# Input projection of a two-layer step: two load queues, x turned one feature tile at a time, the norm applied from PSUM

## The chip, the cores and the metric

The kernel runs on one core of a Trainium2 chip. Times are device microseconds (us) of one execution. The kernel before takes 849.61 us, the median of three runs (848.19 to 850.14).

The engines have short names here: PE is TensorE (matrix products and transposes), PEld its weight loads, DVE is VectorE, ACT is ScalarE, POOL is GpSimd, and SP is the engine that issues loads and stores. An engine that issues a load does so in its own order of instructions: what stands behind the issue waits until it is out.

## The reference, cut to what matters

One step of a model with two layers, all in float32. There are 128 context tokens (x_prompt) and 512 latent tokens (x_sample), each with 1024 features. Layer 0 is latent attention, layer 1 a gated chunk MLP. The change touches the first step of layer 0, the input projection:

```python
sh_c, sc_c, g_c = modulation(c_ctx, w_mod[layer], b_mod[layer])   # silu(cond) @ w_mod + b_mod
sh_l, sc_l, g_l = modulation(c, w_mod[layer], b_mod[layer])
hc = rmsnorm(xc, norm_g[layer]) * (1.0 + sc_c) + sh_c
hl = rmsnorm(xl, norm_g[layer]) * (1.0 + sc_l) + sh_l
proj = h @ w_in             # for hc and hl
c_q, c_kv, k_pe, z = split(proj, [512, 256, 64, 1024])
```

Behind it come the norms of c_q and c_kv, attention, the output projection, layer 1 and the final norm. None of them changes.

## The kernel before, in words

The 640 tokens are five token tiles of 128 (tile 0 is the prompt), the 1024 features eight feature tiles of 128. Large operands are split in two: a part H that is rounded to the type fp32r, and the rest L. A product is then three products of TensorE, one behind the other (`mm3`, L149 to L151: H by H, H by the other's L, L by H), a "triplet".

The order in the code around the change is this. SP issues the five tiles of x (`load_x`, L174) and between them seven small loads of rows (`load_rows`, L183): c, c_ctx, b_mod and some gains. TensorE turns the rows into columns (L201), and VectorE and ScalarE make silu(c) of them. Then come the pieces of w_mod: `PIECES` cuts the eight feature tiles into six pieces (four of one tile, two of two). `mod_piece` loads a piece with four loads (L231) and multiplies it with silu(c) (L236; the trace records each of these float32 products twice); `mod_cols` copies the result to SBUF (L249), turns it (L251) and makes from it the gain and the offset of each feature (`acol`, `modc`, L256 to L272). `load_tok` loads 832 columns of attn_w_in for one feature tile (L290) and splits them (L144 on ScalarE, L145 on VectorE).

Meanwhile x is normed: ScalarE squares and sums each tile (L300), VectorE and GpSimd form the root, VectorE scales the tile in place (L304), for the last tile ScalarE does (L306). Then TensorE turns all of x, 40 transposes of 128x128 (L311), and ScalarE copies them from PSUM to SBUF (L318; L315 and L316 for one tile). `h_piece` applies gain and offset to a feature tile (L330, in place) and splits it.

The loop at the end (L529) goes over the pieces. In each turn it prepares the next piece, and multiplies the present one: for each token tile the 512 columns of c_q (`tok_mm` with kv 0, 128x512), and for token tiles 0 and 1 the 320 columns of c_kv and k_pe too (kv 1, 128x320). The sums of kv 0 stay in PSUM banks 0 to 4, those of kv 1 go to banks 5 to 7. Behind the loop come the last piece, all kv 1 products of token tiles 2 to 4, and each tile's norm.

The order of each engine's instructions is fixed when the program is built: a scheduler interleaves what the code lists, and each engine then works its list off in order. Loads share eight signal lanes: a load that gets a lane which an earlier load holds is issued only when that one has landed.

Of the kernel before, what the change touches and what calls it, by code (L numbers as in the profile page):

```python
# [7 lines left out]
F32 = mybir.dt.float32  # L8
F32R = mybir.dt.float32r
AF = mybir.ActivationFunctionType  # L10
ALU = mybir.AluOpType
AX = mybir.AxisListType

P = 128
D = 1024
KD = D // P
NT = 5
TOK = NT * P
# [35 lines left out]
F_X = 0  # L54
F_Y = 5120
F_MOD = 10496
# [3 lines left out]
C_BMOD = 0  # L60
C_NG = 48
C_VG = 64
C_VB = 80
C_QG = 96
C_C = 100
# [29 lines left out]
def _program(tc, nc, i, o, sb, ps, dr):  # L95
    arR = sb.tile([P, R_N], F32R, name="arR")[:]
    arF = sb.tile([P, F_N], F32, name="arF")[:]
    ident = sb.tile([P, P], F32, name="ident")[:]
    cst = sb.tile([P, C_N], F32, name="cst")[:]
    silc = sb.tile([P, 16], F32, name="silc")[:]  # L100
    modc = sb.tile([P, 2, 24, 2], F32, name="modc")[:]
    acol = sb.tile([P, 2, 8, 2], F32, name="acol")[:]
# [17 lines left out]
    def F(a, n):  # L120
        return arF[:, a : a + n]
# [4 lines left out]
    def F3(at, cnt, **kw):  # L126
        return arF[:, at : at + cnt].rearrange("p (a b) -> p a b", **kw)

    arP = ps.tile([P, 4096], F32, name="arP")[:]
# [10 lines left out]
    V, S, T, G = nc.vector, nc.scalar, nc.tensor, nc.gpsimd  # L140

    def split(h, l, x):

        S.copy(h, x)  # L144
        V.tensor_tensor(l, x, h.bitcast(F32), ALU.subtract)  # L145
# [7 lines left out]
    def rstd(out, ss, n):  # L153

        V.tensor_scalar(out, ss, 1.0 / n, EPS, ALU.mult, ALU.add)  # L155
        G.tensor_tensor(out, out, nhalf, ALU.pow)  # L156
# [3 lines left out]
    def col(n=1):  # L160
        if scol[0] + n > 96:
            scol[0] = 0
        a = scol[0]
        scol[0] += n
        return st[:, a : a + n]
# [7 lines left out]
    def load_x(t):  # L173
        nc.sync.dma_start(F(F_X + t * D, D), x_src[t])  # L174

    def load_rows(name, at, n):
        src = i[name]
        src = (
            src.rearrange("(k p) -> k p", p=P)
            if len(src.shape) == 1  # L180
            else src.rearrange("a (k p) -> (a k) p", p=P)
        )
        nc.sync.dma_start(arF[at : at + n, F_MOD : F_MOD + P], src)  # L183

    load_x(0)
    load_rows("c", C_C, 8)
    load_rows("c_ctx", C_C + 8, 8)
    load_x(1)
    load_rows("b_mod", C_BMOD, 48)
    load_rows("norm_g", C_NG, 16)  # L190
    load_x(2)
    load_rows("mlp_v_norm_g", C_VG, 16)
    load_rows("mlp_v_norm_b", C_VB, 16)
    load_rows("attn_q_norm_g", C_QG, 4)
    load_x(3)
    load_x(4)
    make_identity(nc, ident)
    V.memset(nhalf, -0.5)

# [14 lines left out]

    PIECES = [(0, 1), (1, 1), (2, 1), (3, 1), (4, 2), (6, 2)]
    raw = Ring(F_MOD + 896, F_N)
    raw2 = Ring(F_X, F_X + 5120)

    def wmod(layer, c0, n, k0, nk):
        return i["w_mod"][layer, k0 * P : (k0 + nk) * P, c0 : c0 + n].rearrange(  # L220
            "(k p) n -> p k n", p=P
        )

    def mod_piece(k0, nk, second):


        n = 2 * nk * P
        for kk in range(2):
            a = (raw2 if second and kk else raw).take(4 * n)
            for part in range(2):  # L230
                nc.sync.dma_start(  # L231
                    F3(a, 4 * n, a=4)[:, :, part * nk * P : (part + 1) * nk * P],
                    wmod(0, part * D + k0 * P, nk * P, 4 * kk, 4),
                )
            for j in range(4):
                T.matmul(  # L236
                    arP[32 * j : 32 * j + 32, 3584 : 3584 + n],
                    s32[:, 4 * kk + j, :],
                    F(a + j * n, n),
                    start=kk == 0,  # L240
                    stop=kk == 1,
                    tile_position=(0, 32 * j),
                )
# [49 lines left out]
        wtok.append((R(w, TCOLS), R(w + TCOLS, TCOLS)))  # L293


    xnT = F3(F_Y, 5120, a=KD)
    for t in range(NT):
        x = F(F_X + t * D, D)
        ss = col()
        S.activation(F(F_Y + t * D, D), x, AF.Square, accum_out=ss)  # L300
        r = col()
        rstd(r, ss, D)
        if t < NT - 1:
            V.tensor_scalar(x, x, r, None, ALU.mult)  # L304
        else:
            S.activation(x, x, AF.Identity, scale=r)  # L306
    for t in range(NT):
        x = F(F_X + t * D, D)
        pt = arP[:, t % 3 * 1024 : t % 3 * 1024 + 1024]
        for k in range(KD):  # L310
            T.transpose(pt[:, k * P : (k + 1) * P], x[:, k * P : (k + 1) * P], ident)  # L311
        dst = xnT[:, :, t * P : (t + 1) * P]
        pt = pt.rearrange("p (k n) -> p k n", n=P)
        if t == 3:
            S.copy(dst[:, :4], pt[:, :4])  # L315
            V.tensor_copy(dst[:, 4:], pt[:, 4:])  # L316
        else:
            S.copy(dst, pt)  # L318

    def hT(k):  # L320
        a = R_HT + k * 1280
        return R(a, 640), R(a + 640, 640)

    def h_piece(k0, nk, t0=0, t1=NT):
        for k in range(k0, k0 + nk):
            h = xnT[:, k, :]
            H, L = hT(k)
            for c, a, b in ((1, t0 * P, P), (0, max(t0, 1) * P, t1 * P)):
                if a < b:
                    V.tensor_scalar(  # L330
                        h[:, a:b],
                        h[:, a:b],
                        acol[:, 0, k, c : c + 1],
                        modc[:, 0, k, c : c + 1],
                        ALU.mult,
                        ALU.add,
                    )
            sl = slice(t0 * P, t1 * P)
            split(H[:, sl], L[:, sl], h[:, sl])

# [3 lines left out]
    def tok_mm(t, ks, kv):  # L346
        out = PKV[t] if kv else PQ[t]
        sl = slice(512, TCOLS) if kv else slice(0, 512)
        for k in ks:
            mm3(  # L350
                out,
                [z[:, t * P : (t + 1) * P] for z in hT(k)],
                [z[:, sl] for z in wtok[k]],
                k == 0,
                k == KD - 1,
            )
# [167 lines left out]

    load_tok(0)
    mod_cols(*PIECES[0])
    h_piece(0, 1, 0, 2)
    h_piece(0, 1, 2, NT)
    for q, (k0, nk) in enumerate(PIECES):  # L529
        ks = range(k0, k0 + nk)  # L530
        if q + 1 < len(PIECES):
            mod_piece(*PIECES[q + 1], True)
            mod_cols(*PIECES[q + 1])
            h_piece(*PIECES[q + 1])
            for k in range(PIECES[q + 1][0], sum(PIECES[q + 1])):
                load_tok(k)
            for t in range(NT):
                tok_mm(t, ks, 0)
                if t < 2:
                    tok_mm(t, ks, 1)  # L540
    nc.sync.dma_start(kvg, i["attn_kv_norm_g"].partition_broadcast(P)[:, 0, :])
    for t in range(NT):
        tok_mm(t, ks, 0)
        tok_mm(t, ks if t < 2 else range(KD), 1)
        tok_norm(t)
        if t >= 2:
            tok_turn(t - 2)
# [822 lines left out]
    ss = [col(4) for t in range(NT)]  # L1370
# [14 lines left out]
    for t in range(NT):  # L1385
        x = x_half(t, 0)
# [6 lines left out]
    for t in range(NT):  # L1393
        x = x_half(t, 1)
# [75 lines left out]
```

## Time and profile before

| | |
|---|---|
| median of three runs | 849.61 us (848.19 to 850.14) |
| the profiled execution | 848.43 us |
| its span, first to last instruction | 846.6 us |
| busy in the span: PE / PEld / DVE / ACT / POOL | 812.5 / 741.5 / 640.6 / 408.9 / 18.1 us |
| bytes moved by loads and stores | 131.14 MB, mean 155 GB/s |

The profile is of one execution; its rows give starts from the beginning of the span. A busy time on PE is modelled: products are pipelined, and a product's row is longer than the step to the next one. So steps from start to start are used for prices. The granted clock is a share of 2.4 GHz: 1.00 is that, 0.50 is 1.2 GHz; where no change has been recorded yet, at the start, the view shows 1.00.

### The profile page before, as it was taken

What the parts mean: (1) busy time and instruction counts of PE and PEld (TensorE: products, weight loads), DVE (VectorE), ACT (ScalarE), POOL (GpSimd) and SP (SyncE); (2) the same over time, 40 slices, a digit from 0 to 9 for tenths busy, and PEclk for the clock granted to TensorE, in tenths of its full rate; (3) what the DMA queues carried; (4) which work ended last, traced back from release to release, by engine and by line L of the source; (5) the groups of instructions that cost most, each with busy time, mean ns of one, the idle gap of its engine ahead of it and who ended that gap; (6) DMA issues with size and microseconds to landing.
All of it is one profiled execution on the core that took longest, in us unless ns stands there. A gap on an engine that the chain in (4) does not pass through costs nothing.

```text
span 846.6 us, 12750 instructions
## 1 busy us (share of the span) xinstructions
PE 812.5 (96%) x4874; PEld 741.5 (88%) x4874; DVE 640.6 (76%) x1133; ACT 408.9 (48%) x720; POOL 18.1 (2%) x31
## 2 busy tenths in 40 slices
PE   4999999999999999999999979999999999889996
PEld 3779999999999998888878779999999999668886
DVE  3665997879899896568866778998888787775432
ACT  6344362867666783244323376455455454642111
POOL 1001000000000000000000000000000000000000
PEclk9999999999999999999999989999999999999999
DMA  9981574111223137456869467534425366762212
GB/s 282 298 277 33 168 227 152 26 51 60 85 76 100 37 117 271 133 174 202 264 209 289 136 216 243 174 119 140 156 83 173 104 210 200 227 196 87 63 64 74
DMA packets 115734, 131.14 MB, mean 155 GB/s; under 512 B 5564, under 2 KB 81880, under 8 KB 115416
## 3 DMA queue, kind: packets, MB, share of 16 engines
q1 hardware_dynamic: 115672, 130.32, 49.3%
q8 instruction: 38, 0.62, 0.3%
q14 instruction: 24, 0.20, 0.1%
HBM read 106.78 MB, written 23.52 MB: 154 GB/s over the span
## 4 chain that ended last, share of the span: by engine, by line
PE 70%; DVE 12%; DMA 9%; issue 4%; ACT 3%; POOL 1%; SPq 0%; POOLq 0%; DVEq 0%; ACTq 0%
PE arP L1200 19%; PE arP L149 13%; PE arP L151 13%; PE arP L150 13%; PE arP L736 6%; DVE arR L145 3%; DMA arF<-d_h 2%; PE arP L764 2%; DVE arF L485 2%; DMA arF<-in_mlp_w_in 2%; DMA arF<-d_t 1%; ACT arR L144 1%; PE arP L1245 1%; PE arP L236 1%; PE arP L1246 1%
## 5 line engine op out<-in xcount | busy, mean ns | idle before, releaser
L149 PE MATMUL arP<-arR 128*128 128x512 f32 (+3 forms) x840 | 299.2, 357 | 8.6 <-ACT arR L144 8.0
L150 PE MATMUL arP<-arR 128*128 128x512 f32 (+3 forms) x840 | 297.6, 354 | 2.1 <-DVE arR L145 2.1
L151 PE MATMUL arP<-arR 128*128 128x512 f32 (+3 forms) x840 | 295.9, 354 | 0.0
L144 ACT CAST arR<-arF 128x1024 fp32r<-128x1024 f32 (+5 forms) x199 | 166.0, 854 | 190.0 <-PE arP L1200 31.6
L145 DVE TENSOR_TENSOR arR<-arF,arR 128x512 fp32r<-128x512 f32 (+5 forms) x199 | 190.8, 974 | 52.2 <-ACT arR L144 50.5
L1200 PE MATMUL arP<-arR 128*128 128x320 f32 x1344 | 203.3, 312 | 4.6 <-ACT arF L1274 3.8
L1200 PEld LDWEIGHTS arP<-arR 128*128 128x128 f32 x1344 | 200.0, 190 | 5.3 <-ACT arF L1274 4.1
L149 PEld LDWEIGHTS arP<-arR 128*128 128x128 f32 x840 | 158.4, 189 | 30.4 <-ACT arR L144 11.2
L150 PEld LDWEIGHTS arP<-arR 128*128 128x128 f32 x840 | 158.9, 189 | 20.7 <-DVE arR L145 3.6
L151 PEld LDWEIGHTS arP<-arR 128*128 128x128 f32 x840 | 158.7, 189 | 19.4 <-issue 0.8
L485 DVE SCALAR_TENSOR_TENSOR arF<-arF,silc 128x512 f32<-128x512 f32 x112 | 77.7, 743 | 2.5 <-DMA arF<-in_w_mod 2.5
L145 DVE TENSOR_TENSOR arR<-arP,arR 128x512 fp32r<-128x512 f32 (+4 forms) x86 | 54.7, 685 | 11.8 <-ACT arR L144 11.6
L736 PE MATMUL arP<-arR 128*128 128x320 f32 (+1 forms) x360 | 54.5, 308 | 0.1
L144 ACT CAST arR<-arP 128x512 fp32r<-128x512 f32 (+4 forms) x86 | 45.9, 605 | 16.5 <-PE arP L151 11.3
L736 PEld LDWEIGHTS arP<-arR 128*128 128x128 f32 x360 | 51.9, 188 | 0.4 <-DVE arR L699 0.4
L752 ACT ACTIVATE arF<-arP,st 128x640 f32<-128x640 f32 (+1 forms) x40 | 28.0, 701 | 23.4 <-DVE st L751 22.6
L1381 DVE TENSOR_TENSOR arF<-arP,arF 128x512 f32<-128x512 f32 (+1 forms) x11 | 6.8, 638 | 33.1 <-PE arP L151 33.1
L756 ACT ACTIVATE arF<-arF,st 128x640 f32<-128x640 f32 (+1 forms) x40 | 28.9, 743 | 2.3 <-DVE st L755 1.9
L748 DVE TENSOR_REDUCE st<-arP 128x1 f32<-128x640 f32 (+1 forms) x40 | 28.1, 708 | 1.7 <-PE arP L736 1.0
L1383 ACT ACTIVATE arF<-arF 128x512 f32<-128x512 f32 (+1 forms) x11 | 6.5, 588 | 45.3 <-DVE arF L1382 45.3
L1278 ACT COPY arF<-arP 128x320 f32<-128x320 f32 x16 | 6.8, 425 | 39.6 <-PE arP L1200 39.6
L156 POOL TENSOR_TENSOR st<-st,nhalf 128x1 f32<-128x1 f32 x15 | 10.1, 671 | 643.5 <-DVE st L155 331.6
(154 smaller groups left out, 682.2 us busy)
## 6 DMA issues: line engine op xcount, KB each, us to landing
arF<-in_mlp_w_in SPq DMA_DIRECT2D x48, 512.0 KB, 4.4
arF<-in_w_mod SPq DMA_DIRECT2D x40, 512.0 KB, 4.5
arF<-in_mlp_w_o SPq DMA_DIRECT2D x32, 256.0 KB, 3.3
arR<-d_vh SPq DMA_DIRECT2D x8, 640.0 KB, 4.5
d_t<-arF SPq DMA_DIRECT2D x16, 320.0 KB, 2.9
arF<-d_t SPq DMA_DIRECT2D x16, 320.0 KB, 3.9
arF<-in_x_sample SPq DMA_DIRECT2D x8, 512.0 KB, 4.8
arF<-in_w_mod SPq DMA_DIRECT2D x16, 256.0 KB, 6.1
```

Of the source, the lines that this page charges most:

```text
L144: S.copy(h, x)
L145: V.tensor_tensor(l, x, h.bitcast(F32), ALU.subtract)
L149: T.matmul(out, a[0], b[0], start=start, stop=False)
L150: T.matmul(out, a[0], b[1], start=False, stop=False)
L151: T.matmul(out, a[1], b[0], start=False, stop=stop)
L485: V.scalar_tensor_tensor(acc[:, c, :], w, sc, acc[:, c, :], ALU.mult, ALU.add)
L736: T.matmul(p[:, n0 : n0 + n], a[:, qs], b[:, c0 : c0 + n], start=s0, stop=s1)
L748: V.tensor_reduce(c[:, 0:1], sc, AX.X if q == 0 else AX.XY, ALU.max)
L752: S.activation(pv, sc, AF.Exp, bias=c[:, 0:1], scale=SCALE, accum_out=c[:, 1:2])
L756: S.activation(pr, pr, AF.Identity, scale=c[:, 2:3])
L764: T.transpose(p[:, at : at + P], PR[q][:, kt * P : (kt + 1) * P], ident)
L1200: T.matmul(out, x, y, start=first and k + j == 0, stop=k == 3 and j == 2, skip_group_check=True,)
```

## The change

- The loads are spread over two queues. SP issues the five tiles of x first, one behind the other. ScalarE issues the seven loads of rows and the four loads of the first piece of w_mod, ahead of all its other work.
- Eight products of zeros (128x256) are put in front on TensorE.
- The squares of x go to PSUM instead of SBUF, and the second ring of load buffers (`raw2`) lies in the free part of F_Y instead of x's own place.
- x stays in SBUF as it was normed. `h_piece` turns one feature tile of all five token tiles (L318, 5 transposes) into banks 5 and 6 of PSUM. VectorE makes h from there (L330), ScalarE makes the rounded H from there too (L331), and VectorE subtracts the two for L (L332). The copies L315, L316 and L318 of before go.
- All kv 1 products, for all token tiles, come behind the loop, since banks 5 and 6 are in use during it.

```diff
-    def load_rows(name, at, n):
+    def load_rows(name, at, n, eng=nc.sync):
...
-        nc.sync.dma_start(arF[at : at + n, F_MOD : F_MOD + P], src)
-
-    load_x(0)
-    load_rows("c", C_C, 8)
-    load_rows("c_ctx", C_C + 8, 8)
-    load_x(1)
...
-    load_x(3)
-    load_x(4)
+        eng.dma_start(arF[at : at + n, F_MOD : F_MOD + P], src)
+
+    for t in range(NT):
+        load_x(t)
+    load_rows("c", C_C, 8, nc.scalar)
+    load_rows("c_ctx", C_C + 8, 8, nc.scalar)
...
+    load_rows("attn_q_norm_g", C_QG, 4, nc.scalar)
+
+    zero = F(F_Y, 256)
+    V.memset(zero, 0.0)
+    for _ in range(8):
+        T.matmul(arP[:, 2048:2304], zero[:, :P], zero, start=True, stop=True)
...
-    raw2 = Ring(F_X, F_X + 5120)
+    raw2 = Ring(F_Y + 1280, F_Y + 5120)
...
-                nc.sync.dma_start(
+                (nc.sync if second else nc.scalar).dma_start(
...
-        S.activation(F(F_Y + t * D, D), x, AF.Square, accum_out=ss)
+        S.activation(arP[:, t % 2 * D : t % 2 * D + D], x, AF.Square, accum_out=ss)
...
-    for t in range(NT):
-        x = F(F_X + t * D, D)
-        pt = arP[:, t % 3 * 1024 : t % 3 * 1024 + 1024]
-        for k in range(KD):
-            T.transpose(pt[:, k * P : (k + 1) * P], x[:, k * P : (k + 1) * P], ident)
-        dst = xnT[:, :, t * P : (t + 1) * P]
-        pt = pt.rearrange("p (k n) -> p k n", n=P)
-        if t == 3:
-            S.copy(dst[:, :4], pt[:, :4])
-            V.tensor_copy(dst[:, 4:], pt[:, 4:])
-        else:
-            S.copy(dst, pt)
...
-    def h_piece(k0, nk, t0=0, t1=NT):
+    def h_piece(k0, nk):
+
         for k in range(k0, k0 + nk):
-            h = xnT[:, k, :]
+            for t in range(NT):
+                at = 2560 + (t - 1) * P if t else 3072
+                T.transpose(
+                    arP[:, at : at + P],
+                    arF[:, F_X + t * D + k * P : F_X + t * D + (k + 1) * P],
+                    ident,
+                )
+            h = F(F_Y + k % 2 * TOK, TOK)
             H, L = hT(k)
...
-            split(H[:, sl], L[:, sl], h[:, sl])
+            for c, sl, p in (
+                (1, slice(0, P), arP[:, 3072 : 3072 + P]),
+                (0, slice(P, TOK), arP[:, 2560:3072]),
+            ):
+                g, s = acol[:, 0, k, c : c + 1], modc[:, 0, k, c : c + 1]
+                V.tensor_scalar(h[:, sl], p, g, s, ALU.mult, ALU.add)
+                S.activation(H[:, sl], p, AF.Identity, bias=s, scale=g)
+            V.tensor_tensor(L, h, H.bitcast(F32), ALU.subtract)
...
             for t in range(NT):
                 tok_mm(t, ks, 0)
-                if t < 2:
-                    tok_mm(t, ks, 1)
...
         tok_mm(t, ks, 0)
-        tok_mm(t, ks if t < 2 else range(KD), 1)
+        tok_mm(t, range(KD), 1)
```

The scheduler orders each engine's instructions anew. On TensorE, from the first piece of w_mod (L236) to the first products of the projection (L149, L150), there stood before:

```order
L236 MATMUL arP<-arF 32x256 x4
L311 MATMUL arP<-ident,arF 128x128 x8
L236 MATMUL arP<-arF 32x256 x4
L311 MATMUL arP<-ident,arF 128x128 x8
L251 MATMUL arP<-ident,arF 128x128 x2
L236 MATMUL arP<-arF 32x256 x4
L149 MATMUL arP<-arR 128x512
L236 MATMUL arP<-arF 32x256 x4
L150 MATMUL arP<-arR 128x512
L149 MATMUL arP<-arR 128x320
```

Here the four groups of L236 are the two halves of piece 0 and the two of piece 1; the first product stands ahead of the second half of piece 1, and all transposes of x (L311) are done before it. Now the same place reads (L238 is the product of a piece, L253 its transposes, L318 the transposes of x):

```order
L238 MATMUL arP<-arF 32x256 x8
L318 MATMUL arP<-ident,arF 128x128
L253 MATMUL arP<-ident,arF 128x128 x2
L238 MATMUL arP<-arF 32x256 x4
L318 MATMUL arP<-ident,arF 128x128 x2
L238 MATMUL arP<-arF 32x256 x4
L253 MATMUL arP<-ident,arF 128x128 x2
L318 MATMUL arP<-ident,arF 128x128 x2
L149 MATMUL arP<-arR 128x512
L150 MATMUL arP<-arR 128x512
L238 MATMUL arP<-arF 32x256 x4
L318 MATMUL arP<-ident,arF 128x128 x4
```

The first product has moved behind both halves of piece 1 and its transposes; six transposes of x stand ahead of it and 34 behind. On ScalarE the program began like this before, with the squares (L300), the evacuations of transposes (L318, L315), the scaling of the last tile (L306) and the splits (L144):

```order
L300 ACT_TABLE_LOAD
L300 ACTIVATE arF,st<-arF 128x1024 x3
L206 ACTIVATE st<-cst 128x16
L300 ACTIVATE arF,st<-arF 128x1024 x2
L318 COPY arF<-arP 128x8x128
L306 ACTIVATE arF<-arF,st 128x1024
L318 COPY arF<-arP 128x8x128 x2
L315 COPY arF<-arP 128x4x128
L318 COPY arF<-arP 128x8x128
L144 CAST arR<-arF 128x832
L144 CAST arR<-arF 128x256
```

Now it begins with eleven loads, of which the last five are:

```order
L183 DMA arF<-in_attn_q_norm_g 4x128
L233 DMA arF<-in_w_mod 128x4x128 x4
L301 ACT_TABLE_LOAD
L301 ACTIVATE arP,st<-arF 128x1024
L208 ACTIVATE st<-cst 128x16
L301 ACTIVATE arP,st<-arF 128x1024 x3
L144 CAST arR<-arF 128x832
L301 ACTIVATE arP,st<-arF 128x1024
L307 ACTIVATE arF<-arF,st 128x1024
L331 ACTIVATE arR<-arP,modc,acol 128x128
L144 CAST arR<-arF 128x832
L331 ACTIVATE arR<-arP,modc,acol 128x512
```

The squares stand behind the loads, the split of attn_w_in's first tile stands ahead of the last square, the evacuations are gone, and the scalings from PSUM (L331) have come in their place, with a split between the two of the first feature tile.

## Rows read from the trace of the kernel before

**Rows 1.** Busy time by stage: us, PE, PEld, DVE, ACT, POOL, PEclk, DMA share, GB/s

```profile
0.00:20.70 20.70, 9.85 (x68) 7.31 (x68) 7.53 (x26) 13.54 (x21) 3.91 (x11) 1.00 0.91 281
20.70:59.60 38.90, 38.90 (x231) 28.22 (x232) 26.20 (x65) 13.55 (x20) 0.40 (x1) 1.00 0.97 301
59.60:130.00 70.40, 69.82 (x475) 68.18 (x474) 57.48 (x110) 31.95 (x66) 3.25 (x5) 1.00 0.51 151
```

**Rows 2.** The chain of waits in order of time, head: start us, us, what

```profile
1.91 4.75 DMA arF<-in_x_sample
...
15.19 1.15 ACT arF L306
16.34 1.81 ACT arF L318 x2
...
19.55 1.10 ACT arR L144 x2
...
20.70 0.50 PE arP L149
```

**Rows 3.** Busy time by stretch, columns as in rows 1: the head, and around 490

```profile
0.00:4.00 4.00, 0.00 (x0) 0.00 (x0) 0.33 (x2) 1.28 (x1) 0.70 (x6) 1.00 0.51 150
4.00:8.00 4.00, 0.00 (x0) 0.00 (x0) 0.29 (x3) 2.30 (x4) 0.55 (x1) 1.00 0.96 330
8.00:12.00 4.00, 3.16 (x14) 2.63 (x15) 2.61 (x7) 1.53 (x4) 1.56 (x2) 1.00 0.86 281
...
490.00:492.00 2.00, 2.00 (x11) 1.68 (x10) 0.64 (x4) 0.60 (x1) 0.55 (x1) 1.00 1.00 401
```

**Rows 4.** DMA issues by line: count, KB each, median us to landing (13.2 to 15.3; 0 to 75)

```profile
arF<-in_w_mod SPq DMA_DIRECT2D x4, 256.0 KB, 5.3
...
arF<-in_attn_w_in SPq DMA_DIRECT2D x8, 416.0 KB, 6.9
```

**Rows 5.** SP in order of time: start us, us, line, what it issues

```profile
1.17 0.37 SPq L183 DMA_DIRECT2D arF<-in_c  x1
...
13.18 2.08 SPq L231 DMA_DIRECT2D arF<-in_w_mod  x4
```

**Rows 6.** TensorE in order of time: start us, us, line, operation

```profile
11.06 3.52 PE L311 MATMUL arP<-ident,arF 128*128 128x128 f32 x16
...
15.07 1.09 PE L311 MATMUL arP<-ident,arF 128*128 128x128 f32 x8
...
21.13 0.64 PE L236 MATMUL arP<-arF 128*32 128x256 f32 x8
...
22.94 0.39 PE L150 MATMUL arP<-arR 128*128 128x512 f32 x1
23.17 0.38 PE L251 MATMUL arP<-ident,arF 128*128 128x128 f32 x2
23.30 0.48 PE L151 MATMUL arP<-arR 128*128 128x512 f32 x1
23.62 0.31 PE L149 MATMUL arP<-arR 128*128 128x320 f32 x1
...
59.59 0.30 PE L149 MATMUL arP<-arR 128*128 128x320 f32 x1
```

**Rows 7.** Groups by shape, 0 to 20.7: count | busy us, mean ns | idle before

```profile
L300 ACT ACTIVATE arF<-arF 128x1024 f32<-128x1024 f32 x5 | 5.2, 1050 | 3.7 <-DMA arF<-in_x_prompt 2.4 <-DMA arF<-in_x_sample 1.4
...
L306 ACT ACTIVATE arF<-arF,st 128x1024 f32<-128x1024 f32 x1 | 1.1, 1150 | 0.2 <-POOL st L156 0.2
...
L330 DVE TENSOR_SCALAR arF<-arF,acol,modc 128x128 f32<-128x128 f32 x2 | 0.6, 344 | 0.0
...
L249 DVE COPY arF<-arP 128x256 f32<-128x256 f32 x1 | 0.4, 412 | 0.0
```

**Rows 8.** TensorE behind an idle stretch, and the granted clock there (columns as rows 1)

```profile
727.22 0.50 PE L149 MATMUL arP<-arR 128*128 128x512 f32 x1 [3.66 <-ACT arR L144]
...
728.00:730.00 2.00, 2.00 (x7) 1.52 (x6) 1.97 (x6) 2.00 (x7) 0.00 (x0) 0.50 0.53 152
```

More of the change, by code (lines that the diff above doesn't have):

```diff
@@ L182, in load_rows @@
         )
-        nc.sync.dma_start(arF[at : at + n, F_MOD : F_MOD + P], src)
-    load_x(0)
-    load_rows("c", C_C, 8)
-    load_rows("c_ctx", C_C + 8, 8)
-    load_x(1)
[L189 to L194, printed above, removed]
-    load_x(3)
-    load_x(4)
+        eng.dma_start(arF[at : at + n, F_MOD : F_MOD + P], src)
[3 more added lines that the diff above has]
+    load_rows("c_ctx", C_C + 8, 8, nc.scalar)
+    load_rows("b_mod", C_BMOD, 48, nc.scalar)
+    load_rows("norm_g", C_NG, 16, nc.scalar)
+    load_rows("mlp_v_norm_g", C_VG, 16, nc.scalar)
+    load_rows("mlp_v_norm_b", C_VB, 16, nc.scalar)
+    load_rows("attn_q_norm_g", C_QG, 4, nc.scalar)
[3 more added lines that the diff above has]
+        T.matmul(arP[:, 2048:2304], zero[:, :P], zero, start=True, stop=True)
     make_identity(nc, ident)
@@ L293, in load_tok @@
         wtok.append((R(w, TCOLS), R(w + TCOLS, TCOLS)))
-    xnT = F3(F_Y, 5120, a=KD)
     for t in range(NT):
@@ L322, in hT @@
         return R(a, 640), R(a + 640, 640)
-    def h_piece(k0, nk, t0=0, t1=NT):
+    def h_piece(k0, nk):
         for k in range(k0, k0 + nk):
-            h = xnT[:, k, :]
-            H, L = hT(k)
[L328 to L338, printed above, removed]
-            split(H[:, sl], L[:, sl], h[:, sl])
+            for t in range(NT):
[6 more added lines that the diff above has]
+            h = F(F_Y + k % 2 * TOK, TOK)
+            H, L = hT(k)
+            for c, sl, p in (
[6 more added lines that the diff above has]
+            V.tensor_tensor(L, h, H.bitcast(F32), ALU.subtract)
     PQ = [arP[:, t * 512 : (t + 1) * 512] for t in range(NT)]
@@ L526, in _program @@
     mod_cols(*PIECES[0])
-    h_piece(0, 1, 0, 2)
-    h_piece(0, 1, 2, NT)
+    h_piece(0, 1)
     for q, (k0, nk) in enumerate(PIECES):
```

## The prediction

> **What bounds the kernel now.** I read the busy time by stage first. Up to 20.7 us TensorE is busy for 9.85 us, and little of that is products of the projection; from 20.7 to 59.6 us it is busy for all 38.90 us, and from there to 130 us for 69.82 of 70.40 us [rows 1]. So the stretch that the change touches has two parts with different limits: a head in which TensorE waits, and a stretch in which nothing but its own work counts. The chain of waits names what the head waits for: after the loads come the scaling of the last token tile on ScalarE, three evacuations of transposed x, the casts of h, and then the first product at 20.70 us [rows 2]. A gain has to come out of the head; whatever TensorE has to do after 20.7 us costs its full time.
>
> The point to compare at is a product that both programs share. From the 128x320 product of token tile 1 at feature tile 6, which starts at 59.59 us [rows 6], TensorE's order is the same in both programs to the end, and those of the other engines join within the same few products. TensorE is almost never idle for the next 70 us [rows 1]. So the change in the time is the change in when that product starts. In both programs 34 triplets of 128x512 and 14 of 128x320 stand between the first product of the projection and it.
>
> **The first product: what has to land.** In the changed order TensorE reaches its first product only behind all products of pieces 0 and 1 with w_mod (before: without the second half of piece 1). SP issues the five x tiles and attn_w_in of feature tile 0 ahead of piece 1. So five x tiles of 128x1024 float32 (512 KB each), eight w_mod loads of 256 KB, one of 416 KB [rows 4] and 58 KB of rows have to be in: 5.20 MB. These are the same bytes that lie ahead of the end of piece 1 before, where its four loads were issued from 13.18 to 15.26 us and landed 5.3 us later at the median [rows 4, 5]: the last at about 20.1 us. The second queue moves issue times, not bytes. The DMA engines were already 96% busy from 4 to 8 us at 330 GB/s, with one queue, and had a dip to 281 GB/s from 8 to 12 us [rows 3], while x waited for its place. Two queues can fill that dip: 4 us x 49 GB/s = 0.2 MB, or 0.6 us. I take 19.4 us. Bounds: 0.60 MB by 4 us [rows 3], the other 4.60 MB at 330 GB/s and no delay from last byte to signal, gives 17.9 us; nothing gained gives 20.1 us.
>
> The Trainium skill ("DMA: Bandwidth & Descriptors", section "Issuing engines are not separate DMA queues") says that transfers from several engines end on the same 16 DMA engines and interleave, so that a second issuer saves only issue time. By that rule the landing stays near 20.1 us; the trace agrees so far as one queue reaches a share of 0.96 to 1.14.
>
> **From landing to the first product.** The half of piece 1 on TensorE 0.64 us [rows 6], the copy of its rows 0.41, two transposes beside it, the gain and offset columns about 0.2, the first 128x128 scaling on VectorE 0.34 [rows 7], then the same on ScalarE, which waits for VectorE's reading; no row has it, 0.27 to 0.4 by its neighbour on VectorE. With the hand-overs 2.2 us: first product at 21.6 us, against 20.70. Behind it the tiles of x_sample need the 128x512 scaling on both engines in turn, and ScalarE has a cast of 128x832 queued ahead of it: tile 1 starts some 2.2 us after tile 0, of which TensorE fills 1.6 with two products, a piece and transposes. Idle: 0.6 us.
>
> ScalarE's own chain is not last by this count. It issues 11 loads of about 0.4 us each [rows 5] from 0.74 us and waits for the second x tile (landed at 6.66 us before [rows 2]); then a table load, five squares of 1.05 plus read-out, one cast of 128x832 and one scaling of 1.15 [rows 7] bring it to 17.7 us, or 19.6 where x lands late, and it is needed at 21.0. The evacuations removed there (L315, L318) were on the path before [rows 2]; what is late next is the w_mod piece.
>
> **The dense stretch.** Before: 59.59 - 20.70 = 38.9 us. The products are the same. Gone are one half piece (0.6 us) and two transposes. Added are 34 transposes of x, 128x128, which before were done in the head. Their price stands in the trace: L150, two transposes, L151 take 22.94 to 23.62 us, where the two products alone take 0.46, so 0.11 us each at the full clock [rows 6]; 34 x 0.11 = 3.7 us. The stretch is 38.9 - 0.6 - 0.2 + 3.7 = 41.8 us. The 128x320 products of tiles 0 and 1 move from the loop to its end, at no cost or gain, since TensorE does as many of them by the shared point. The loop per feature tile is then 5 x 3 x 0.23 for products, 0.55 for transposes, about 1.2 for the piece and 0.22 for its transposes: 5.4 us, where its loads (1.44 MB at 330 GB/s) take 4.4 us. So loads stay hidden, as does the scaling on VectorE and ScalarE; if that cover fails once per piece by half a microsecond it costs 3 us.
>
> Sum: 19.4 + 2.2 + 0.6 + 41.8 = 64.0 us, against 59.6: **+4.4 us** before the clock. Each microsecond of landing moves it by one.
>
> **The clock.** The eight products of zeros run at the start, from about 1.2 us, and are done by 8 us; nothing waits for them. What they could buy is the full clock. Before, the transposes from 11.06 us step at 0.22 us and those from 15.07 us at 0.11 [rows 6]: TensorE stood at 1.2 GHz, and rose to 2.4 only behind sixteen of them that filled 3.5 us without a break. After, transposes come one by one as x arrives, and between 8 and 19 us TensorE has about 2 us of work. Later in the trace it idles for 3.66 us ahead of a product at 727.22 us and is granted half the clock just behind it, 0.50 over 728 to 730 us [rows 8]; a product then steps at 0.43 us, which over 3.4 us loses 1.7 us. So the warm start is likely lost again before it is of use. Bounds 0 and 3.4 us (twice such a stretch); the row nearest to it gives 1.7, of which part falls into time in which TensorE waits anyway: I take 1.2.
>
> **Forecast: slower by 5.6 us.** On the profiled execution (span 846.6, 848.43 us in all) that is 854.0 us; the runs' median is 849.61, which gives 855.2.
>
> **Rivals.**
> - *The two queues together draw more, and the time stays.* For it: 401 GB/s stands in the trace from 490 to 492 us [rows 3]. Then the 4.60 MB take 11.5 us, landing is at 15.5 us, and the sum 15.5 + 2.2 + 0.6 + 41.8 is 60.1: +0.5 us, if the clock is full too, 850.1 us. It decides from a landing before 16.7 us; for faster it would have to be before 13.3. Against: no stretch of 4 us in the head goes over 330 GB/s [rows 3], and rows of 512 bytes make up the pieces.
> - *Piece 0 starves on its own queue.* Its 512-byte rows compete with the 4 KB rows of x, so it lands with piece 1 instead of well before; its copy, its transposes and the scalings of x queued between them on VectorE then stand ahead of piece 1, some 1.3 us, and TensorE idles more, so the clock costs 3.4: +4.4 + 1.3 + 3.4 = +9.1, 858.7 us. SP's wait for piece 0 ahead of each next load speaks against a worse case. The Trainium skill ("DMA: Bandwidth & Descriptors", section "Queues, rings and completion order") has the DMA engines take turns between queues by whole packets, which would favour large rows; no trace of one queue shows it.
> - *The clock stays full.* The forecast without its last term: +4.4, 854.0 us. It is inside the forecast's range.
> - *The warm-up or the second queue do nothing at all*: the landing at 20.1 us, +5.1 and the clock: 855.9 us, also inside.
>
> **Chances.** Forecast with its two variants 0.70 (853.0 to 857.5), no change by faster loads 0.10, starved piece 0.15, something not seen here 0.05, split between faster and much slower. A change under 0.2%, 1.7 us, can't be told from none in this kernel. Faster 0.05, within 0.10, slower 0.85. The range reaches from 850.8 to 859.8: the lower end cuts into the case of faster loads, the upper end takes in the starved piece.
>
> **What would show it.** The first 128x512 product near 21.6 us; the shared 128x320 product near 64 to 65.5; forty transposes in place of L311, 34 of them between those two at 0.11 us; a granted clock of 0.50 somewhere between 15 and 26 us; a DMA share near 1 without the dip at 8 to 12 us. ScalarE's scaling of the last x tile before the end of piece 1 shows that loads are the bound. I am wrong if the first product starts before 18 us, or if the shared product follows it by much other than 42 to 44 us; the part after the shared product should keep its length to within a microsecond.

## Result and profile after

The changed kernel takes 862.44 us, the median of four runs (860.79 to 864.19), against 849.48 for the kernel before: a ratio of 1.016, 95% interval 1.0136 to 1.0183. It is slower, as forecast, but by 13 us and not by 5.6, and the time lies above the range. The profiled execution has a span of 862.1 us, against 846.6.

Up to the product that both programs share (the 128x320 product of token tile 1 at feature tile 6), the stages are now these. Columns: us, then busy time (and instructions) of PE, PEld, DVE, ACT, POOL, the granted clock, DMA share, GB/s.

```profile
0.00:25.18 25.18, 13.96 (x59) 7.31 (x60) 7.58 (x30) 9.45 (x16) 3.45 (x11) 0.69 0.91 278
25.18:73.55 48.37, 46.09 (x256) 32.13 (x257) 28.67 (x63) 18.29 (x30) 0.70 (x1) 0.95 0.75 230
73.55:143.95 70.40, 69.83 (x476) 68.34 (x475) 55.61 (x105) 30.71 (x63) 2.96 (x4) 1.00 0.48 136
```

Beside [rows 1] the head is 4.48 us longer (25.18 for 20.70) and the dense stretch 9.47 (48.37 for 38.90); the next 70 us behind the shared product keep their length to 0.1 us (the products run in the same order in both, and each comes 13.9 to 14.0 us later). So 13.96 of the 15.5 us in the span lie ahead of 73.55 us, where the prediction looked. The other 1.5 us come late, where this execution had more stretches at half clock than the one of before. Two of the other three runs were 3 us under it, so I give that part no cause in the change. The dense stretch also lost its density: TensorE is idle for 2.3 us of it, and the DMA share fell from 0.97 to 0.75.

The head on TensorE, in order of time (start us, us; in brackets the idle time before and what ended it; L198 are the products of zeros, L238 a half piece of w_mod, L318 transposes of x):

```profile
1.18 6.21 PE L198 MATMUL arP<-arF 128*128 128x256 f32 x16 [1.18 <-DVE arF L196]
7.23 0.26 PE L203 MATMUL arP<-ident,arF 116*128 116x116 f32 x1
13.68 0.47 PE L318 MATMUL arP<-ident,arF 128*128 128x128 f32 x1 [6.18 <-DVE arF L305]
...
18.05 1.08 PE L238 MATMUL arP<-arF 128*32 128x256 f32 x8 [1.39 <-DMA arF<-in_w_mod]
...
20.68 1.08 PE L238 MATMUL arP<-arF 128*32 128x256 f32 x8 [0.33 <-DVE modc L258]
...
22.42 1.08 PE L238 MATMUL arP<-arF 128*32 128x256 f32 x8
...
24.61 0.92 PE L318 MATMUL arP<-ident,arF 128*128 128x128 f32 x2
25.18 0.78 PE L149 MATMUL arP<-arR 128*128 128x512 f32 x1
```

A half piece takes 1.08 us here, where it took 0.64 [rows 6]: TensorE is at 1.2 GHz. The clock by stretch (columns as above):

```profile
8.00:12.00 4.00, 0.00 (x0) 0.00 (x0) 0.00 (x0) 2.42 (x4) 0.00 (x0) 0.71 0.97 330
12.00:16.00 4.00, 0.89 (x6) 0.41 (x9) 2.17 (x8) 3.32 (x8) 1.57 (x3) 0.50 1.12 338
...
24.00:28.00 4.00, 3.95 (x17) 1.96 (x18) 3.69 (x11) 2.55 (x4) 0.00 (x0) 0.50 0.99 298
28.00:32.00 4.00, 4.00 (x16) 3.18 (x14) 2.57 (x3) 2.01 (x3) 0.00 (x0) 0.73 1.05 324
```

The products of zeros end at 7.4 us; behind one transpose of the rows TensorE is idle for 6.18 us, and the clock that they had bought is back at half before 12 us. It stays there until 30.15 us, 5 us into the dense stretch.

What the head waits for stands on VectorE (L155 a root's first step, L305 the scaling of an x tile, L251 the copy of a piece's result, L145 a split of attn_w_in):

```profile
15.31 0.14 DVE L155 TENSOR_SCALAR st<-st 128x1 f32<-128x1 f32 x1
19.18 0.42 DVE L251 COPY arF<-arP 128x256 f32<-128x256 f32 x1 [3.73 <-PE arP L238]
19.53 0.74 DVE L305 TENSOR_SCALAR arF<-arF,st 128x1024 f32<-128x1024 f32 x1
20.19 0.14 DVE L155 TENSOR_SCALAR st<-st 128x1 f32<-128x1 f32 x1
...
20.99 0.75 DVE L305 TENSOR_SCALAR arF<-arF,st 128x1024 f32<-128x1024 f32 x1 [0.36 <-POOL st L156]
21.66 1.02 DVE L145 TENSOR_TENSOR arR<-arF,arR 128x832 fp32r<-128x832 f32 x1
22.60 0.15 DVE L155 TENSOR_SCALAR st<-st 128x1 f32<-128x1 f32 x1
```

VectorE stands for 3.73 us at the copy of piece 0, with the scalings of two x tiles behind it in its queue, and behind these a split of attn_w_in (1.02 us) and then the root of the last x tile (22.60). On ScalarE this comes out as:

```profile
5.51 4.03 ACTq L233 DMA_DIRECT2D arF<-in_w_mod  x4
...
10.87 1.03 ACT L301 ACTIVATE arP<-arF 128x1024 f32<-128x1024 f32 x1
...
23.41 1.15 ACT L307 ACTIVATE arF<-arF,st 128x1024 f32<-128x1024 f32 x1 [5.42 <-POOL st L156]
24.55 0.46 ACT L331 ACTIVATE arR<-arP,modc,acol 128x128 fp32r<-128x128 f32 x1
```

ScalarE is held by its own four load issues from 5.51 to 9.54 us, so the first square stands at 10.87 us, behind the table load. The last x tile, squared by 18 us, is scaled at 23.41. Its first transpose (24.61) stands ahead of the first product in TensorE's order, so the first product waits for that scaling. Piece 0 itself is late. The loads of w_mod that were issued up to 25 us, by queue (count, KB each, median us from issue to landing):

```profile
arF<-in_w_mod SPq DMA_DIRECT2D x12, 256.0 KB, 4.8
...
arF<-in_w_mod ACTq DMA_DIRECT2D x4, 256.0 KB, 10.0
```

The row of SP is of later pieces. The loads of piece 0 itself, in the kernel before:

```profile
arF<-in_w_mod SPq DMA_DIRECT2D x4, 256.0 KB, 6.5
```

So piece 0's four loads take 10.0 us at the median on ScalarE's queue, and took 6.5 on SP's. The last lands at 17.91 us; in the kernel before it landed at 15.53. Piece 1 ends at 20.20 us, before at 20.19: nothing was gained there.

Last, the loop, around the last piece of w_mod, and the shared product:

```profile
49.09 0.39 PE L151 MATMUL arP<-arR 128*128 128x512 f32 x1
50.90 1.02 PE L238 MATMUL arP<-arF 128*32 128x512 f32 x2 [1.43 <-DMA arF<-in_w_mod]
...
73.55 0.31 PE L149 MATMUL arP<-arR 128*128 128x320 f32 x1
```

TensorE comes to the last piece at 49.3 us and waits for it. In the kernel before it began that piece at 44.58 us and waited for nothing.

### The profile page after: what moved, and what is told of

Same layout as the page of the kernel before. It is cut to its first block, busy times and chain, and to the rows that moved or that the text cites. A ratio compares the mean times of both kernels' runs of the same rounds, so it can differ in the third digit from the quotient of the medians.

```text
span 862.1 us, 12787 instructions
## 1 busy us (share of the span) xinstructions
PE 825.7 (96%) x4890; PEld 746.9 (87%) x4890; DVE 642.5 (75%) x1131; ACT 408.1 (47%) x722; POOL 17.6 (2%) x31
## 3 DMA queue, kind: packets, MB, share of 16 engines
q10 hardware_dynamic: 2312, 1.11, 0.5%
## 4 chain that ended last, share of the span: by engine, by line
PE 71%; DMA 12%; DVE 9%; issue 4%; ACT 3%; POOL 0%; SPq 0%; ACTq 0%; POOLq 0%; DVEq 0%
PE arP L1190 20%; PE arP L149 13%; PE arP L151 12%; PE arP L150 12%; PE arP L726 6%; DMA arF<-d_h 2%; DVE arR L145 2%; DMA arF<-in_w_mod 2%; PE arP L754 2%; DMA arF<-in_mlp_w_in 2%; DVE arF L478 1%; ACT arR L144 1%; DMA arF<-d_t 1%; PE arP L238 1%; PE arP L1235 1%
## 5 line engine op out<-in xcount | busy, mean ns | idle before, releaser
L149 PE MATMUL arP<-arR 128*128 128x512 f32 (+3 forms) x840 | 301.8, 360 | 6.5 <-ACT arR L144 5.5
L150 PE MATMUL arP<-arR 128*128 128x512 f32 (+3 forms) x840 | 299.1, 356 | 3.4 <-DVE arR L145 3.4
L144 ACT CAST arR<-arF 128x1024 fp32r<-128x1024 f32 (+4 forms) x190 | 160.1, 862 | 178.6 <-PE arP L1190 33.0
L145 DVE TENSOR_TENSOR arR<-arF,arR 128x1024 fp32r<-128x1024 f32 (+4 forms) x190 | 184.6, 986 | 49.1 <-ACT arR L144 47.6
L149 PEld LDWEIGHTS arP<-arR 128*128 128x128 f32 x840 | 159.8, 190 | 27.3 <-ACT arR L144 6.1
L150 PEld LDWEIGHTS arP<-arR 128*128 128x128 f32 x840 | 160.0, 191 | 21.7 <-DVE arR L145 4.4
L145 DVE TENSOR_TENSOR arR<-arP,arR 128x512 fp32r<-128x512 f32 (+4 forms) x86 | 54.7, 687 | 11.0 <-ACT arR L144 10.9
L144 ACT CAST arR<-arP 128x512 fp32r<-128x512 f32 (+4 forms) x86 | 46.0, 606 | 16.4 <-PE arP L151 12.6
```

The lines of the kernel that those rows point to most:

```text
L149: T.matmul(out, a[0], b[0], start=start, stop=False)
L150: T.matmul(out, a[0], b[1], start=False, stop=False)
```

## Experiments

All times below are read at two points of each kernel's own profile, the first 128x512 product and the shared product, beside the timed ratio to the kernel before on the same chip.

| kernel | first product | shared product | ratio, 95% interval |
|---|---|---|---|
| before | 20.70 | 59.59 | 1 |
| changed | 25.18 | 73.55 | 1.016 (1.0136 to 1.0183) |
| changed, all loads on SP as before | 21.43 | 67.05 | 1.0108 (1.0079 to 1.0138) |
| changed, more products to keep TensorE busy | 23.68 | 66.49 | 1.0088 (1.0053 to 1.0123) |
| both of these | 22.82 | 67.71 | 1.0085 (1.0062 to 1.0108) |
| changed, no products of zeros | 25.44 | 73.08 | 1.0156 (1.0115 to 1.0197) |
| changed, VectorE's order repaired | 23.17 | 68.98 | 1.0109 (1.008 to 1.0139) |
| changed, piece 0 on SP | 19.50 | 65.74 | 1.0062 (1.0034 to 1.009) |
| piece 0 on SP, 16 more zeros | 20.27 | 66.59 | 1.0056 (1.0034 to 1.0077) |
| piece 0 on SP, full clock throughout | 21.14 | 65.50 | 1.0086 (1.0066 to 1.0106) |
| before, with the changed loads | 27.68 | 66.16 | 1.0099 (1.0068 to 1.0129) |
| before, x first, rows on ScalarE | 23.54 | 62.34 | 1.0008 (0.9987 to 1.0028) |
| before, smaller second ring | 21.07 | 60.29 | 1.000 (0.9979 to 1.002) |
| before, 128x320 products put last in the code | 21.41 | 61.13 | 1.0018 (1.0002 to 1.0034) |
| before, 128x320 products held back | 20.42 | 62.96 | 1.0039 (1.0019 to 1.0058) |

A profile is one execution: two rows with ratios near 1.000 have the shared product 0.7 and 2.75 us later. Differences of that size are read from the ratios. In the last row the order behind the loop is another one (one triplet of token tile 2 comes early); the point taken there is the one with as many products of the projection done, 144.

**The loads, undone in the changed kernel and put alone into the kernel before.**

```
-    load_rows("c", C_C, 8, nc.scalar)
+    load_rows("c", C_C, 8)
...
-                (nc.sync if second else nc.scalar).dma_start(
+                nc.sync.dma_start(
```

(and the other rows likewise, between the x tiles as before; for the kernel before the same lines with - and + exchanged)

> The changed kernel with its loads issued as before: all on SP, x and the small rows in turns, piece 0 of w_mod behind x on SP; the rest stays changed. Changed: 862.4 us, first 128x512 product at 25.2 us, shared product at 73.5. Queue theory (piece 0 on ScalarE's queue lands at 17.9 us instead of 15.5, and what hangs on it makes most of the loss above the forecast): first product at 21 to 22.5 us, time 855 to 858. Clock theory (half clock from 9.7 to 30.2 us because TensorE has little to do in the head): first product not before 23.5 us, half clock into 27 us or later, time 859 to 861. Work theory (34 transposes, fewer load buffers and more waits behind the first product): from first to shared product still 46 to 48 us.

> The kernel before with only its loads changed: x first on SP, rows and piece 0 issued by ScalarE. Before: 849.5 us. Queue theory: slower by 4 to 7 us, 854 to 856, with piece 0 in at about 18 us and the first product at 24 or later. Clock theory: its dense transposes of x bring the clock up all the same, so at most 1 to 2 us slower, 850 to 851.5. Work theory: 849.5, no change.

Undone, they give back 6.50 us at the shared product. Put alone into the kernel before, they cost 6.57. By the ratios the first is 4.4 us and the second 8.4. Piece 0 is late there too: its last load lands at 16.97 us, and VectorE stands 3.38 us at its copy with an x tile behind it. Its loads there, by queue:

```profile
arF<-in_w_mod SPq DMA_DIRECT2D x10, 256.0 KB, 5.0
...
arF<-in_w_mod ACTq DMA_DIRECT2D x4, 256.0 KB, 8.7
```

So the way that the loads are split costs about half of the loss, with the other edits and without them.

**The clock.** More products of zeros behind the first transpose, and one product per x tile:

```
+    for _ in range(16):
+        T.matmul(arP[:, 2048:2304], zero[:, :P], zero, start=True, stop=True)
...
+        T.matmul(arP[:, 2048:2304], ident, x[:, :256], start=True, stop=True)
```

> The changed kernel with 16 more products of zeros behind the transpose of the rows and one product of the identity with 256 columns of x behind each tile's norm, all to a free bank of PSUM, so that TensorE is busy through most of the head. Clock theory: full clock when the first product comes, first product 1 to 2 us earlier, from first to shared product 2 to 2.5 us shorter, time 858 to 859.5. Queue theory: first product where it was (25 us), 860 to 861. Work theory: 862 to 863, the added products only cost.

Against it, the changed kernel without any such product:

```
-    for _ in range(8):
-        T.matmul(arP[:, 2048:2304], zero[:, :P], zero, start=True, stop=True)
```

> The changed kernel without its eight products of zeros. The clock rose at 6.3 us and fell again at 9.7, long before the first product. Clock theory as put in the prediction (the warm start is lost before it is of use): 862.4, within 1.5 us. Rival (the zeros do help): half clock beyond 30 us and 864 or more. Second rival (they stand in the way of the transpose of the rows on TensorE, 7.2 us): 861 or less.

And the keep-busy products together with all loads on SP, as in the first pair:

> The changed kernel with both repairs: loads in the order and on the queue of the kernel before, and the keep-busy products (16 products of zeros and one 128x256 product per x tile) on TensorE. By my own sum (full clock, 41.8 us from first to shared product; with one queue the first product measured 21.4 us) the shared 128x320 product starts near 64.2 us, +4.6 over the kernel before: ratio about 1.0055, some 852.7 us. If the two gains add up (6.5 us for one queue and 7.1 for the clock, each measured alone against the changed kernel), the shared product is near 60.0 and the time that of the kernel before (ratio 1.000, 848.5). If the clock was only a matter of the two queues, nothing changes against the one-queue kernel: 67 us, ratio 1.011.

The first gained 7.06 us, which looked like the clock. But with all loads on SP the same products gained nothing at the shared product (67.71 against 67.05; the ratios' intervals overlap), although TensorE had its full clock there from 5.7 us on:

```profile
20.00:24.00 4.00, 2.98 (x28) 1.40 (x24) 3.08 (x9) 1.28 (x3) 0.00 (x0) 1.00 1.09 284
```

The stretch behind the first product was 0.73 us shorter, but the first product came 1.39 us later. What the runs that gained have in common is something else: in all of them the scheduler had put the copy of piece 0 behind the x scalings on VectorE. The clock theory falls in this form; it had got its support from a changed order. Without the products of zeros the time is the same as with them (1.0156 and 1.016): they buy nothing that these runs can show.

**VectorE's order by itself.** The copy of piece 0 gets an operand made from x tiles 2 and 3 (their first columns times zero), so it can't stand ahead of their scalings; both queues stay:

```
+    one = col()
+    V.tensor_scalar(one, F(F_X + 3 * D, 1), F(F_X + 2 * D, 1), 0.0, ALU.mult, ALU.mult)
-    mod_cols(*PIECES[0])
+    mod_cols(*PIECES[0], one)
...
+            V.tensor_scalar(rows, pt, one, None, ALU.add)
```

> The changed kernel, both queues as they are, with VectorE's order repaired: a one-column product of x tiles 2 and 3 with zero is added to the copy of piece 0, so that this copy stands behind the scalings of all x tiles on VectorE instead of ahead of those of tiles 2 and 3. Order theory (in the changed kernel VectorE stands 3.73 us at the copy, until piece 0 is in, with two x tiles behind it; the runs that gained 7 us, all loads on SP and the keep-busy products, had this order too): last x tile scaled near 20.5 us instead of 24.5, shared product at 66.5 to 68, ratio 1.008 to 1.010. Clock theory (the keep-busy products gained by the clock): the clock stays at half up to about 30 us, at most 2 us come back, shared product at 71.5 or later, ratio 1.014.

VectorE and ScalarE, in order of time (L308 scales an x tile, L254 is the copy, L310 scales the last x tile):

```profile
15.84 0.75 DVE L308 TENSOR_SCALAR arF<-arF,st 128x1024 f32<-128x1024 f32 x1 [0.66 <-POOL st L156]
...
19.95 0.48 DVE L254 TENSOR_SCALAR arF<-arP,st 128x256 f32<-128x256 f32 x1 [2.24 <-PE arP L238]
```

```profile
18.25 1.15 ACT L310 ACTIVATE arF<-arF,st 128x1024 f32<-128x1024 f32 x1 [1.07 <-POOL st L156]
```

The last x tile is scaled 5.2 us earlier (18.25 for 23.41), and 4.57 us come back at the shared product (4.3 by the ratios), between what the two theories said and nearer to the order theory. The clock rose earlier too (at 22.7 us instead of 30.15), after TensorE had begun to work almost without a break (3.88 of the 4 us from 20 us). So the 4.57 us are not the order's alone: 2.01 stand at the first product, and 2.56 in the stretch behind it, where the half clock was gone. Another thing differed that the edit had not asked for: the last of ScalarE's four issues took 0.5 us and not 2.5, so the first square stood at 8.80 us instead of 10.87. What that gave isn't separated.

**Piece 0 on SP, the rows still on ScalarE's queue.** 

```
-                (nc.sync if second else nc.scalar).dma_start(
+                nc.sync.dma_start(
```

> The changed kernel with piece 0 of w_mod issued from SP; the seven row loads stay on ScalarE's queue. If the piece starving on its own queue is what costs (starvation theory): piece 0 lands by 16 us instead of 17.9, first product near 21.4 us instead of 25.2, shared product near 67, ratio to the kernel before about 1.010, as with all loads on SP. If ScalarE's late squares (10.9 us, behind its blocked issues) are the cost, the same, since they move with it; the squares then stand at 5 to 10 us. If the order of x ahead of the rows is the cost, nothing is gained: shared product near 73, ratio 1.016.

The median time to landing of w_mod falls back (6.7 us for the four loads of piece 0), and both points move by more than expected, to 19.50 and 65.74 us:

```profile
arF<-in_w_mod SPq DMA_DIRECT2D x16, 256.0 KB, 6.2
```

These four loads cost 7.8 us of the 13.96, of which the order on VectorE that they led to is up to 4.6. The late landing and ScalarE's late squares (5.95 us here, 10.87 before the edit) moved together in this run, so they are not told apart. What is left, 6.15 us, is close to the forecast's 5.6, and the ratio of 1.0062 to its 1.0066. That closeness is luck: the first product stands at 19.50 us and not at 21.6, and the stretch to the shared product takes 46.24 us and not 43.6 (41.8, 0.6 and 1.2).

**The clock again, without piece 0 in the way.** Piece 0 on SP, the 16 products of zeros from above, and in the second run also:

```
     mod_cols(*PIECES[0])
+    for _ in range(5):
+        T.matmul(arP[:, 2048:2304], ident, F(F_X + 4 * D, 256), start=True, stop=True)
```

> The changed kernel with piece 0 issued from SP (first product 19.5 us, shared product 65.7 us, half clock from 10.5 to 24.3 us) and 16 more products of zeros on TensorE, none of which waits for a load. Clock theory: TensorE has the full clock at its first products, the 4.8 us of the dense stretch at half clock give 2.4 us back, shared product near 63.4, which is my sum without the clock (64.0). Ratio near 1.004. If the lost time at half clock is hidden behind loads, the shared product stays at 65.7, ratio 1.006; if the products of zeros stand in the way of piece 0 on TensorE, it is later.

> As the run with 16 products of zeros and piece 0 from SP, whose clock fell at 18.6 us, and five more products (identity by 256 columns of x tile 4, about 0.22 us each at full clock) in TensorE's gap between the two pieces, at about 17.3 us. If they hold the full clock over the first products, the half-clock term can be read by itself: shared product at 63.4 to 64.2 instead of 65.7 us, ratio near 1.0045. If the clock falls anyway, or if the loop's loads take back what it gains, shared product 65.5 to 67 and ratio 1.0055 to 1.007.

In the first the clock fell to half at 18.6 us all the same, so it tells nothing of the clock. In the second (five products of x tile 4 between the pieces) it was full all through:

```profile
16.00:20.00 4.00, 4.00 (x33) 2.68 (x25) 2.64 (x9) 1.77 (x3) 0.00 (x0) 1.00 1.16 313
20.00:24.00 4.00, 3.80 (x29) 2.75 (x26) 3.15 (x10) 1.89 (x3) 0.00 (x0) 1.00 1.18 310
```

Yet the shared product stood at 65.50 instead of 65.74, and the ratio was no better (1.0086 for 1.0062). The stretch was 1.89 us shorter, but the first product came 1.64 us later, and TensorE then waited for the last piece (L240 is its product, on SP the issue of its loads):

```profile
45.37 1.06 PE L240 MATMUL arP<-arF 128*32 128x512 f32 x8 [1.71 <-DVE arR L334]
```

```profile
37.47 2.67 SPq L235 DMA_DIRECT2D arF<-in_w_mod  x4
```

The releaser named in the first row had long been done: the loads of that half, issued from 37.47 us, landed at 43.74 and 45.24. In the kernel before the same half landed at 44.04, TensorE began it at 44.58 and had not waited: it had been busy up to then, with six products of 128x320 among its work since 40.4 us. From the start of the last piece to the shared product it took 15.01 us there, with 18 products of 128x320 in it. In both kernels of this kind it takes 20.13, with 42 of them. The 24 more products at 0.145 us are 3.5 of the 5.1 us between these, and 14 transposes at 0.11 the other 1.5.

**The 128x320 products moved in the kernel before.** First by the code's order alone:

```
-                if t < 2:
-                    tok_mm(t, ks, 1)
...
-        tok_mm(t, ks if t < 2 else range(KD), 1)
+        tok_mm(t, range(KD), 1)
```

> The kernel before, with the 128x320 products of token tiles 0 and 1 moved out of the loop to its end, as in the changed kernel; nothing else. By the prediction this is free: TensorE does as many of them by the shared product, which stays at 59.6 (ratio 1.000, within 0.002). If the loop without them is shorter than its loads (cover theory), TensorE waits for pieces of w_mod in the loop by 1 to 3 us: ratio 1.001 to 1.004, idle time on in_w_mod between 36 and 56 us.

Beside it the other thing that the change does to the loop's loads, their smaller ring:

```
-    raw2 = Ring(F_X, F_X + 5120)
+    raw2 = Ring(F_X, F_X + 3840)
```

> The kernel before with the second ring of load buffers cut from 5120 to 3840 columns, the size in the changed kernel; nothing else. If the smaller ring is what makes loads late in the loop (ring theory), TensorE waits for pieces there by 1 to 2 us, ratio 1.001 to 1.003. If not, the shared product stays at 59.6 us and the ratio at 1.000 within 0.002.

The ring is free, as expected. The other run decided nothing, since the scheduler put the products back into the loop: 23 of the 24 stood in it as before, and 19 instead of 18 behind the last piece. So they were held there, by two products of the last feature tile's h into their PSUM banks:

```
+    for b in (5, 6):
+        z = hT(KD - 1)[0][:, :P]
+        T.matmul(arP[:, b * 512 : b * 512 + P], z, z, start=True, stop=True)
```

> The kernel before with the 128x320 products of token tiles 0 and 1 held behind the loop (two 128x128 products of the last feature tile's h are put into their PSUM banks ahead of them, so that none can run earlier); the earlier try left 19 of 24 where they had been. By the prediction the place of these products is free: shared product at 59.6 to 60.0 us, ratio 1.000. By the cover theory the last piece of w_mod cannot start before its loads are in, near 44.5 us, and what is held back stands behind it: 24 products of 0.145 us, 3.5 us more from the last piece to the shared product (18.5 instead of 15.0), TensorE idle ahead of that piece, shared product near 63, ratio 1.0035 to 1.0045.

```profile
42.15 1.07 PE L236 MATMUL arP<-arF 128*32 128x512 f32 x8 [0.30 <-DMA arF<-in_w_mod]
44.70 0.50 PE L149 MATMUL arP<-arR 128*128 128x512 f32 x1 [1.49 <-ACT arR L144]
...
62.96 0.31 PE L151 MATMUL arP<-arR 128*128 128x320 f32 x1
```

The place of the products is not free: 3.4 us at the point with as many of them done, 3.3 at the first 128x512 product behind token tile 2's 128x320 products (69.34 for 66.04), ratio 1.0039 (1.0019 to 1.0058). TensorE is now idle for 2.1 us between the first product and that point, where it never was before. But the way is not quite the one that the cover theory named. The last piece started at 42.15 us and waited only 0.30 for its load; the longest wait, 1.49 us, was for ScalarE's casts of h of the piece before. What the products had covered was the making of h as much as the loads.

**The best form of the loads, in the kernel before.** Five x tiles first on SP, the rows on ScalarE's queue, piece 0 on SP.

```
+    for t in range(NT):
+        load_x(t)
+    load_rows("c", C_C, 8, nc.scalar)
...
```

> The kernel before with one part of the change: five x tiles first on SP, the seven row loads on ScalarE's queue, piece 0 stays on SP. In the changed kernel this form of the loads gave the earliest shared product (65.7 us against 67.0 with all loads in the old order). If that carries over, the last x tile lands 1 us earlier, the first product stands near 20.0 us instead of 20.7 and the ratio is 0.999, at best 0.998; if the head is bound by ScalarE's squares and copies, or ScalarE's row issues delay them, it is 1.000 to 1.002.

The last x tile landed at 12.02 us, against 12.24 before, so 0.2 us earlier and not 1. The time did not move. No run here beat the kernel before.

## Why the prediction was wrong

- **The bound and the point to compare at: right.** All but 1.5 us of the difference lies ahead of the shared product. Of the 8.4 us that the forecast missed there (13.96 for 5.6), 3.6 lie ahead of the first product (25.18 for 21.6) and 4.8 in the stretch (48.37 for 43.6).
- **The landing: right, at its upper bound.** Piece 1 ended at 20.20 us (19.4 taken, 20.1 the bound). The dip was not filled, it moved: 287 GB/s from 4 to 8 us instead of 281 from 8 to 12. No stretch of 4 us in the head went over 338 GB/s. The rival in which two queues draw more is out.
- **From landing to the first product: the step that failed first.** It took 4.98 us and not 2.2. I counted what stands behind piece 1 and took the norm of x as done by 17.7 to 19.6 us. The changed order on VectorE had the copy of piece 0 ahead of two x scalings, and piece 0 came late, so the last scaling ended at 24.56 us. This is the rival *piece 0 starves on its own queue*: its mechanism was right and had a chance of 0.15. Its price, +9.1 with 1.3 for what stands behind the copy, was too low: the four loads, with all that follows from them, cost 7.8 us (73.55 to 65.74). The argument against a worse case, SP's waits, looked at the wrong engine: VectorE's queue made it worse. The Trainium skill ("DMA: Bandwidth & Descriptors", section "Queues, rings and completion order") has the DMA engines take turns between queues by whole packets. The trace fits that: from 9 to 13 us the two queues moved about as many rows (361 and 464 records), but SP's (q1) with its large rows 1.23 MB and ScalarE's (q10) 0.23:

```profile
q1 hardware_dynamic: 361, 1.23, 81.8%
q10 hardware_dynamic: 464, 0.23, 19.6%
```

- **"The 128x320 products move at no cost or gain": wrong.** I counted work up to a common point. But they covered waits in the loop, for loads and for h, and the count holds only while TensorE never waits. Held back in the kernel before, they cost 3.4 us there.
- **"Loads stay hidden": wrong for the same reason.** TensorE idles 2.3 us in the stretch, 1.43 of it ahead of the last piece's load and the rest for H and L of h. I had 3 us for a cover that fails, and did not take it.
- **The transposes: right.** Time from their start to the next instruction's, summed between the two points: 1.11 us for 14 transposes before, 5.21 for 48 in the run with more products to keep TensorE busy, whose clock was full there, so 0.12 us each (0.11 taken).
- **The clock: right that the warm start is lost, wrong in length.** Half clock held from 9.7 to 30.15 us; over the first 5 us of the stretch the steps cost 2.3 us more than at the full clock (1.2 taken, 0 to 3.4 the bounds). It isn't a term to add, though: with the full clock and piece 0 on SP the loop waited longer for its last piece (1.71 us).

Against the stretch of 42.81 us in the run with more products to keep TensorE busy (full clock but for the head, VectorE's order good), the changed kernel's 48.37 is made of 2.3 for half clock, 1.6 ahead of the last piece and 1.2 in two steps at 64.2 and 65.5 us that wait for H and L of h; 0.4 is not placed. Open is how the 6.15 us with piece 0 on SP divide. The first product is 1.20 us earlier than in the kernel before and the stretch 7.35 longer, but 3.4 for the held products (measured in the kernel before), 4.1 for the transposes and about 2 for the half clock (an estimate from the 2.3 above) make more than that. That some transposes and some half clock fall into the waits is likely and not shown.

## What to carry to other kernels

A load that is moved to another engine's queue is to be followed to its first reader, and from there to what stands behind that reader in its engine's order: here one copy on VectorE held up two x tiles. Work that is moved "behind the loop" counts as free only if nothing in the loop was waiting behind it; find the last load of the loop and ask what TensorE does until it lands and until its result is made. And an edit that adds instructions to test one cause can change the scheduler's order and so test another: compare the orders before believing the gain.

## What the runs showed of the hardware

- Four loads of 256 KB in 512-byte rows, issued by ScalarE while SP's 4 KB rows were under way, took 10.0 us at the median (8.7 in the kernel before with these loads), against 6.5 and 6.7 for the same four loads on SP (kernel before; piece 0 on SP). ScalarE was held by the last of these issues from 7.07 to 9.54 us; in two other runs the same issue took 0.5 us.
- Eight products of zeros gave the full clock at 6.3 us; idle from 7.5 us, TensorE was at half by 9.7 and stayed there through 20 us of scattered work.
- The clock column reads 1.00 where no record stands yet. Without the products of zeros the first record is at 28.9 us; the row below says 1.00, yet the first product in that stretch runs as long as at half clock:

```profile
24.00:28.00 4.00, 3.69 (x16) 1.71 (x17) 3.70 (x12) 2.81 (x4) 0.00 (x0) 1.00 1.01 292
```

```profile
25.44 0.77 PE L149 MATMUL arP<-arR 128*128 128x512 f32 x1
```
